# Hybrid attention layer on one core: the output copy on VectorE with three places, and one more key pair as split products

## The chip, the core and the metric

The kernel runs on one core of a Trainium2 chip. The time is the device time of one execution in microseconds (us), median of several runs. Five engines work in parallel, each through its own instructions in order: PE (TensorE, matrix products into the accumulator memory PSUM), DVE (VectorE), ACT (ScalarE), POOL (GpSimd) and SP (SyncE, which issues most DMA transfers). Semaphores tie them together: an instruction that waits holds up everything behind it on its engine.

## The reference, cut to what matters

One transformer layer for 256 prompt tokens and 2048 latent tokens. The change touches only the attention of the latent tokens: 4 heads, each with two softmax maps over 2560 keys (512 cached and 2048 own), whose weighted difference multiplies the values.

```python
s = jnp.einsum('bqhmd,bkhmd->bhmqk', qblk, k).astype(jnp.float32) * scale
p = jax.nn.softmax(s, axis=-1)
a = p[:, :, 0] - lam * p[:, :, 1]
return jnp.einsum('bhqk,bkhe->bqhe', a.astype(v.dtype), v)
```

After it come a norm per head, the output projection and the MLP; a Fourier branch is mixed in before the projection.

## The kernel before, in words

The program passes through stages on the same core: input projection, attention, output projection, a first and a second MLP stage. Attention runs from about 550 to 1255 us of the profiled span.

Attention works on 32 groups, 4 heads times 8 groups of 256 queries. A group has scores (`fill`, L1081, into PSUM tiles Ss of 512 columns), a maximum of each row (`rowmax`, L1086, on DVE, and `comb`, L1089, which joins five of them and negates), the exponentials (`exp`, L1105, on ACT, into P0s and P1s), the weighted difference (`combine`, POOL), and the product with the values. One group of scores takes four steps: two halves j of the queries times two maps m, with five tiles b of 512 keys in each. The products with the values follow six steps behind, so a step computes the scores of one group and the value products of an earlier one.

Value products go by pairs of key tiles: kb = 0, 2, 4, ..., 18 stands for tiles kb and kb + 1. For a pair, PE turns the weights (`tr`, L1136, four transposes into a PSUM tile pts), ACT copies pts to a rounded high part ahs (`ah`, L1143), DVE subtracts that from pts and leaves the low part als (`al`, L1148), and PE multiplies (`mul`): six products of 256 columns per pair (L95, L96, L97: high by high, low by high and high by low, for both tiles) summed in the PSUM tile po. The values Vs stand as a high and a low part as well. Pairs listed in FULL are different: their ahs is a plain fp32 copy, there is no als, and PE takes two fp32 products with unsplit values (vf4s, vf14s; L1162), each recorded as two passes. For pair 14 the first half of the first product runs one step earlier (`mul_part`, L1169).

The four steps of value products take pairs 0, 2 / 4, 6, 8 / 10, 12 / 14, 16, 18; in the two steps with three pairs, the first one is in FULL.

What is shared, and in what turn: the scores have 5 PSUM tiles (Ss), the turned weights 2 (pts), po is one; ahs and als have 4 places each, and the fp32 copies 2 of their own. Places go round in turn, and whoever takes one waits for all readers of what stood in it. So the third `tr` of a step takes the place of the first, and the fifth `ah` that of the first of the last four.

When a group's products are done, `o1` (L1173) copies po to a tile oTs with two places; then follow squares, a power on POOL, two small transfers through memory, a multiplication on POOL and the store to att (L1210). The last group has an oTs of its own in another pool. In the last two groups, turned weights also use the free Ss tiles.

The order is written out by hand: every call is put in a list with a time in units of a step (T, and u = T/5), the list is sorted, and each engine's instructions are recorded in that order. These times set the order only. In a step that begins at w, `rowmax` of the fifth tile stands at 3.9u, `comb` at 4.55u, the third `tr` at 3.86u, `ah` of three pairs at 3.3u, 3.8u and 4.4u, the value products of the step before at 3.9u.

Of the kernel before, what the change touches and what calls it, by code (L numbers as in the profile page):

```python
# [11 lines left out]
F32 = mybir.dt.float32  # L12
# [7 lines left out]
P = 128  # L20
# [9 lines left out]
LAM_INIT = 0.8 - 0.6 * math.exp(-0.3 * 0)  # L30
GRID_W = 64
TSTEP, AVS = 5.2, 6
FULL = (4, 14)

PSCALE = 512 / math.sqrt(256 * 128)

# [5 lines left out]
def body(tc, a, out):  # L42
    nc = tc.nc
    ctx = ExitStack()
    with ctx:
# [944 lines left out]
        with ExitStack() as c3_:  # L990
# [18 lines left out]
            class Head:  # L1009
# [16 lines left out]
                def load_v(self):  # L1026
# [4 lines left out]
                    if not s:  # L1031
                        for kb in FULL:
                            t = ak.tile([P, 2, P], F32, tag=f"vf{kb}", name=f"vf{kb}{self.nm}")
# [6 lines left out]
            class Group:  # L1040
# [98 lines left out]
                def ah(self, kb):  # L1139
                    full = kb in self.hd.vf  # L1140
                    t = at.tile([P, 512], F32 if full else F32R, tag="af" if full else "ah", name=f"ah{self.nm}_{kb}", bufs=2 if full else 4)

                    (nc.vector.tensor_copy if self.drain and kb == FULL[0] else nc.scalar.copy)(t, self.pt[kb])  # L1143
                    self.A[kb] = [t]
# [24 lines left out]
                    nc.tensor.matmul(self.po[:, 0:P], self.hd.vf[kb][:, 0, :], self.A[kb][0][:, 0:P], start=False, stop=False)  # L1169

                def o1(self):
                    self.oT = self.op.tile([P, 256], F32, tag="oT", name=f"oT{self.nm}", bufs=1 if self.last else 2)
                    nc.scalar.copy(self.oT, self.po[:, 0:256])  # L1173

                def oq(self):
                    self.osq = self.op.tile([P, 256], F32, tag="P1_1" if self.hd.s else "osq", name=f"osq{self.nm}", bufs=1)
# [89 lines left out]
            def add(t, fn, *args):  # L1266
                ev.append((t, len(ev), fn, args))
# [20 lines left out]
            for h in range(H):  # L1288
                hd, hp = Head(0, h), Head(1, h)
                base = h * 32 * T  # L1290
                add(base - 18 * T + 0.7 if h else -3.04 * T, hd.load_k)
                add(base - 14 * T + 0.7 if h else 0.9 * T, hd.load_v)
                add(base + 2 * T + 0.7, hp.load_k)
                add(base + 2 * T + 0.71, hp.load_v)
                gp = Prompt(hp, 0)
                G = [base + (AVS + 4 * g) * T for g in range(8)]
                add(G[1] - 3 * T, gp.qload)
                for j in range(2):
                    for m in range(2):
                        for t, fn in ((0.4, gp.scores), (0.85, gp.rowmax), (2.7, gp.exp)):  # L1300
                            add(G[1 + 2 * j + m] + t * u, fn, j, m)
                    add(G[2 + 2 * j] + 8 * u, gp.combine, j)
                for t, fn, *args in ((0.25, gp.tr, 0), (0.9, gp.ah), (1.4, gp.al), (17.0, gp.mul), (20.85, gp.o1), (24.45, gp.oq),
                                     (25.3, gp.o2), (26.0, gp.o5), (26.05, gp.opow), (29.5, gp.o6), (34.0, gp.o7),
                                     (40.2, gp.o8), (43.0, gp.o9)):
                    add(G[5] + t * u, fn, *args)
                for g in range(hd.ng):
                    gr = Group(hd, g)
                    add(base - (4 if h or g > 1 else 3) * T + 0.6 * u if base else -3.03 * T, gr.qload)
                    for st in range(4):  # L1310
                        j, m = divmod(st, 2)
                        t0 = base + st * T
                        for b in range(hd.nbk):
                            add(t0 - T + (0.76 + 0.66 * b) * u, gr.fill, j, m, b)
                            add(t0 - T + (1.26 + 0.66 * b) * u, gr.rowmax, j, m, b)
                            add(t0 + 0.66 * b * u, gr.exp, j, m, b)
                        add(t0 - 0.45 * u, gr.comb, j, m)
                        if m:
                            add(t0 + (4.5 if gr.last and j else 5.9) * u, gr.combine, j)
                            if gr.last and j:  # L1320
                                add(t0 + T + 5.3 * u, gr.combine_v, j)
                    kbs = list(range(0, hd.nkt, 2))
                    for q in range(4):
                        w = base + (AVS + q) * T
                        if q % 2 == 0:
                            order = [kbs.pop(0) for _ in range(2)]
                            tr_t, ah_t, al_t = [0.7, 2.2], [3.3, 3.8], [4.6, 5.2]
                        else:
                            order = [kbs.pop(0) for _ in range(3)]
                            tr_t, ah_t, al_t = [0.7, 2.2, 3.86], [3.3, 3.8, 4.4], [None, 4.6, 5.2]  # L1330
                        for n, kb in enumerate(order):
                            add(w + tr_t[n] * u, gr.tr, kb)
                            add(w + (2.0 if gr.drain and kb == FULL[0] else ah_t[n]) * u, gr.ah, kb)
                            if al_t[n]:
                                add(w + al_t[n] * u, gr.al, kb)
                            add(w + T + (3.9 + 0.01 * n) * u, gr.mul, kb)
                            if q == 3 and not n:
                                add(w + 3.95 * u, gr.mul_part, kb)
                    w = base + (AVS + 5) * T + 1.0 * u
                    for t, fn in ((0, gr.o1), (8.5, gr.oq), (9.3, gr.o2), (10.0, gr.o5), (10.05, gr.opow), (13.0, gr.o6), (17.5, gr.o7), (24.2, gr.o8), (27.0, gr.o9)):  # L1340
                        if gr.last and t > 1:
                            LASTO.append(fn)
                        else:
                            add(w + t * u, fn)
                    base += 4 * T
# [606 lines left out]
        with ExitStack() as c6:  # L1952
# [52 lines left out]
            for i in range(7):  # L2005
                for k in range(16):
                    n = i * 16 + k
# [7 lines left out]
            with tc.manual_schedule():  # L2015
                pend, NM, loaded, KS = None, 7 * 24, 4, []
                for i in range(7):
                    for b in range(3):
                        ps = [pp.tile([P, 512], F32, tag="ps", name=f"ps{i}_{b}_{j}", bufs=6) for j in range(3)]
                        for k in range(16):  # L2020
                            n, m = i * 16 + k, (i * 3 + b) * 8 + k // 2
# [107 lines left out]
```

## Time and profile before

| | |
|---|---|
| median of 3 runs | 2867.51 us (2867.2 to 2867.67) |
| the profiled execution | 2865.04 us |
| its span, first to last instruction | 2863.3 us |
| mean granted clock of PE | 0.998 |
| PE busy | 2830.0 us (99%) |
| DVE busy | 1982.4 us (69%) |
| ACT busy | 1525.3 us (53%) |
| POOL busy | 1068.7 us (37%) |

The span is what the profile's times count in; the time of the execution has about 2 us around it. Busy times of PE hold pipelined instructions, each counted until its modelled end, so 99% does not say that PE never waits: start times of successive instructions tell more. A line of the timeline gives start, duration, engine, source line, operation, output and inputs, count, and in brackets the idle time before it with what ended it.

### The profile page before, as it was taken

What the parts mean: (1) busy time and instruction counts of PE and PEld (TensorE: products, weight loads), DVE (VectorE), ACT (ScalarE), POOL (GpSimd) and SP (SyncE); (2) the same over time, 40 slices, a digit from 0 to 9 for tenths busy, and PEclk for the clock granted to TensorE, in tenths of its full rate; (3) what the DMA queues carried; (4) which work ended last, traced back from release to release, by engine and by line L of the source; (5) the groups of instructions that cost most, each with busy time, mean ns of one, the idle gap of its engine ahead of it and who ended that gap; (6) DMA issues with size and microseconds to landing.
All of it is one profiled execution on the core that took longest, in us unless ns stands there. A gap on an engine that the chain in (4) does not pass through costs nothing.

```text
span 2863.3 us, 43138 instructions
## 1 busy us (share of the span) xinstructions
PE 2830.0 (99%) x15093; PEld 2462.1 (86%) x15093; DVE 1982.4 (69%) x3357; ACT 1525.3 (53%) x3383; POOL 1068.7 (37%) x855
## 2 busy tenths in 40 slices
PE   8999999999999999999999999999999999999999
PEld 5888888688888888888889999999998888888887
DVE  7777786888888888864477777778775354345554
ACT  4333332788888888853356565556555332333221
POOL 1221223789898898942223333333332000000000
PEclk9999999999999999999999999999999999999999
DMA  7777767431222322147767676667747464445663
GB/s 284 215 213 206 234 202 248 159 109 47 78 74 53 112 54 87 46 121 211 246 218 234 221 247 229 220 219 237 235 168 255 146 203 135 137 144 185 207 204 110
DMA packets 404795, 497.69 MB, mean 174 GB/s; under 512 B 31539, under 2 KB 320672, under 8 KB 401506
## 3 DMA queue, kind: packets, MB, share of 16 engines
q1 hardware_dynamic: 399088, 484.35, 53.4%
q0 software_dynamic: 1936, 7.41, 0.8%
q10 hardware_dynamic: 3554, 3.17, 0.3%
q8 instruction: 119, 1.95, 0.3%
q14 instruction: 98, 0.80, 0.1%
HBM read 317.30 MB, written 179.62 MB: 174 GB/s over the span
## 4 chain that ended last, share of the span: by engine, by line
PE 54%; DVE 1%; DMA 0%; issue 0%; ACT 0%; SPq 0%; POOL 0%; DVEq 0%; POOLq 0%
PE ps L95 8%; PE ps L97 8%; PE ps L96 8%; PE pB L1746 2%; PE pB L1745 2%; PE pB L1744 2%; PE pA L1744 2%; PE pC L1746 2%; PE pA L1745 2%; PE pC L1744 2%; PE pC L1745 2%; PE pA L1746 2%; PE po L97 2%; PE po L95 2%; PE po L96 2%; PE pD L1746 1%
## 5 line engine op out<-in xcount | busy, mean ns | idle before, releaser
L1086 DVE TENSOR_REDUCE mxs<-Ss 128x1 f32<-128x512 f32 x636 | 404.9, 685 | 85.5 <-PE Ss L1081 78.2
L1421 DVE TENSOR_TENSOR sl<-sr,sh 128x768 fp32r<-128x768 f32 x168 | 161.8, 964 | 331.6 <-ACT sh L1420 331.1
L1121 POOL TENSOR_TENSOR P0s<-P0s,P1s 128x1024 f32<-128x1024 f32 (+2 forms) x128 | 377.2, 2947 | 10.7
L1420 ACT CAST sh<-sr 128x768 fp32r<-128x768 f32 x168 | 140.6, 838 | 418.3 <-PE ps L96 418.3
L1786 POOL TENSOR_TENSOR gs<-g,g 128x384 f32<-128x384 f32 x48 | 69.7, 1453 | 469.3 <-ACT g L1756 426.4
L1105 ACT ACTIVATE P1s<-Ss,mxs 128x512 f32<-128x512 f32 x318 | 215.4, 694 | 47.7 <-DVE mxs L1089 43.9
L95 PE MATMUL pj<-wh,hh 128*128 128x512 f32 x576 | 228.9, 397 | 2.0 <-DVE hh L556 2.0
L95 PE MATMUL ps<-thT,sh 128*128 128x512 f32 x585 | 227.6, 389 | 0.0
L96 PE MATMUL ps<-tlT,sh 128*128 128x512 f32 x585 | 227.6, 389 | 0.0
L97 PE MATMUL ps<-thT,sl 128*128 128x512 f32 x585 | 227.6, 389 | 0.0
L96 PE MATMUL pj<-wl,hh 128*128 128x512 f32 x576 | 227.3, 395 | 0.1
L97 PE MATMUL pj<-wh,hl 128*128 128x512 f32 x576 | 225.8, 392 | 0.0
L1105 ACT ACTIVATE P0s<-Ss,mxs 128x512 f32<-128x512 f32 x318 | 214.6, 692 | 4.1 <-DVE mxs L1089 4.0
L1136 PE MATMUL pts<-ident,P0s 128*128 128x128 f32 x1280 | 193.4, 275 | 4.8 <-DVE als L1148 1.8
L1081 PE MATMUL Ss<-KS0s,Qs 128*128 128x512 f32 x636 | 188.8, 418 | 4.9 <-ACT P1s L1105 3.7
L1081 PE MATMUL Ss<-KS1s,Qs 128*128 128x512 f32 x636 | 188.1, 419 | 1.8 <-ACT P0s L1105 1.4
L1136 PEld LDWEIGHTS pts<-ident,P0s 128*128 128x128 f32 x1280 | 152.8, 142 | 36.3 <-issue 4.2
L1755 ACT ACTIVATE g<-uz 128x384 f32<-128x384 f32 x144 | 75.8, 526 | 200.2 <-DVE uz L1778 174.1
L1120 POOL TENSOR_SCALAR P1s<-P1s,tots 128x1024 f32<-128x1024 f32 (+2 forms) x128 | 171.5, 1340 | 5.8
L1148 DVE TENSOR_TENSOR als<-pts,ahs 128x512 fp32r<-128x512 f32 x256 | 163.7, 681 | 10.7 <-ACT ahs L1143 10.6
L1143 ACT CAST ahs<-pts 128x512 fp32r<-128x512 f32 x256 | 146.7, 607 | 40.9 <-PE pts L1136 40.9
L95 PE MATMUL ps<-ophT,sh 128*128 128x512 f32 x423 | 164.7, 389 | 1.1 <-DVE uz L1778 1.1
(536 smaller groups left out, 8012.8 us busy)
## 6 DMA issues: line engine op xcount, KB each, us to landing
sr<-sd SPq DMA_DIRECT2D x84, 768.0 KB, 4.3
a<-in_w SPq DMA_DIRECT2D x184, 256.0 KB, 3.6
sd<-gs SPq DMA_DIRECT2D x192, 192.0 KB, 1.9
sd<-g SPq DMA_DIRECT2D x144, 192.0 KB, 4.0
wm<-in_w_mod SPq DMA_DIRECT2D x32, 512.0 KB, 5.2
Qs<-qd SPq DMA_DIRECT2D x32, 512.0 KB, 5.1
b<-in_w SPq DMA_DIRECT2D x64, 256.0 KB, 4.9
b<-tsum SPq DMA_DIRECT2D x64, 256.0 KB, 4.6
```

What stands on the lines that cost most here:

```text
L95: nc.tensor.matmul(ps, lh, rh, start=first, stop=False)
L96: nc.tensor.matmul(ps, lh, rl, start=False, stop=False)
L97: nc.tensor.matmul(ps, ll, rh, start=False, stop=last)
L1081: nc.tensor.matmul(S[:, :w], self.Q[:, x, m, j * P:j * P + P], self.hd.KS[m][:, b * 512:b * 512 + w], start=(x == 0), stop=(x == 1))
L1086: nc.vector.tensor_reduce(self.mx[j][:, m, b:b + 1], self.S[j, m, b], axis=AX.X, op=ALU.max)
L1105: nc.scalar.activation(dst, S, AF.Exp, bias=self.mx[j][:, m, 6:7], accum_out=self.sm[j][:, m, b:b + 1])
L1120: nc.gpsimd.tensor_scalar(p, p, tot[:, 3:4], 0.0, op0=ALU.mult, op1=ALU.add)
L1121: nc.gpsimd.tensor_add(d, d, p)
L1136: nc.tensor.transpose(pt[:, c:c + P], self.p0[j][:, (kb + t) * P:(kb + t + 1) * P], ident)
L1744: nc.tensor.matmul(ps, wh[:, c], hh[:, k, :], start=first and k == 0, stop=False, skip_group_check=True)
L1745: nc.tensor.matmul(ps, wh[:, c], hl[:, k, :], start=False, stop=False, skip_group_check=True)
L1746: nc.tensor.matmul(ps, wl[:, c], hh[:, k, :], start=False, stop=k == 3, skip_group_check=True)
```

## The change

Three edits. The list FULL loses pair 14: tiles 14 and 15 now take the way of the other pairs, with a rounded high part, a low part on DVE (recorded at 4.1u, just ahead of `comb`) and six products; the fp32 values for them are no longer loaded, and the early half product is gone. `o1` moves from ACT to DVE. oTs gets three places (the last group's own stays one).

```diff
-FULL = (4, 14)
+FULL = (4,)
...
                 def o1(self):
-                    self.oT = self.op.tile([P, 256], F32, tag="oT", name=f"oT{self.nm}", bufs=1 if self.last else 2)
-                    nc.scalar.copy(self.oT, self.po[:, 0:256])
+                    self.oT = self.op.tile([P, 256], F32, tag="oT", name=f"oT{self.nm}", bufs=1 if self.last else 3)
+                    nc.vector.tensor_copy(self.oT, self.po[:, 0:256])
...
-                            tr_t, ah_t, al_t = [0.7, 2.2, 3.86], [3.3, 3.8, 4.4], [None, 4.6, 5.2]
+                            tr_t, ah_t, al_t = [0.7, 2.2, 3.86], [3.3, 3.8, 4.4], [4.1 if q == 3 else None, 4.6, 5.2]
...
-                            if q == 3 and not n:
+                            if kb in FULL and q == 3:
                                 add(w + 3.95 * u, gr.mul_part, kb)
```

Over the program this takes out 96 rows of fp32 products of pair 14 on PE and puts in 192 split ones; DVE gains 32 subtractions and 32 copies; ACT loses 32 copies, and 32 plain copies become rounding ones; SP loses 4 loads; POOL's rows stay as they are.

The places, in group 3 of head 0 (pts_3_18 is the tile of turned weights of group 3, pair 18; the brackets name the engines or transfers that an instruction waits for). First PE, in the fourth step of the group's value products: the third `tr` and the products that follow. Before:

```order
L1081 MATMUL Ss_5_1_0_4_6621<-KS0s_5257,Qs_5_6206 128x512 [waits Activation_49]
L1136 MATMUL pts_3_18_6626<-ident,P0s_3_0_5900 128x128 [waits Activation_49]
L95 MATMUL po<-ahs_3_10_6548,Vs_5315 128x256
L95 MATMUL po<-ahs_3_12_6553,Vs_5315 128x256
L1169 MATMUL po<-ahs_3_14_6619,vf14s_5319 128x128
L1136 MATMUL pts_4_0_6658<-ident,P0s_4_0_6201 128x128 [waits DVE_49,PE_49,Pool_49]
L1162 MATMUL po<-ahs_3_14_6619,vf14s_5319 128x128 [waits Activation_49]
L1162 MATMUL po<-ahs_3_14_6619,vf14s_5319 128x256
L95 MATMUL po<-ahs_3_16_6624,Vs_5315 128x256
```

The same place now:

```order
L1081 MATMUL Ss_5_1_0_4_6632<-KS0s_5257,Qs_5_6214 128x512 [waits Activation_49]
L1136 MATMUL pts_3_18_6637<-ident,P0s_3_0_5903 128x128 [waits DVE_49,PE_49]
L95 MATMUL po<-ahs_3_10_6559,Vs_5315 128x256
L95 MATMUL po<-ahs_3_12_6564,Vs_5315 128x256
L1136 MATMUL pts_4_0_6670<-ident,P0s_4_0_6209 128x128 [waits DVE_49,PE_49,Pool_49]
L95 MATMUL po<-ahs_3_14_6630,Vs_5315 128x256 [waits Activation_49]
L96 MATMUL po<-als_3_14_6656,Vs_5315 128x256
L95 MATMUL po<-ahs_3_16_6635,Vs_5315 128x256
```

The turned weights of pair 18, which take the place of those of pair 14, waited for ACT and now wait for DVE, whose subtraction for pair 14 is the last reader. Then DVE in the same step, now:

```order
L1086 TENSOR_REDUCE mxs_5_1_6599<-Ss_5_1_0_4_6632 128x1 [waits PE_49]
L1148 TENSOR_TENSOR als_3_14_6656<-pts_3_14_6594,ahs_3_14_6630 128x512 [waits Activation_49]
L1089 TENSOR_REDUCE mxs_5_1_6599<-mxs_5_1_6599 128x1 [waits DVE_49]
L1148 TENSOR_TENSOR als_3_16_6661<-pts_3_16_6619,ahs_3_16_6635 128x512 [waits Activation_49]
L1148 TENSOR_TENSOR als_3_18_6665<-pts_3_18_6637,ahs_3_18_6658 128x512 [waits Activation_49]
```

The second row is new; the others stood in this order before. Last ACT at the same place, now:

```order
L1143 CAST ahs_3_14_6630<-pts_3_14_6594 128x512 [waits PE_49,Activation_49]
L1143 CAST ahs_3_16_6635<-pts_3_16_6619 128x512 [waits PE_49,Activation_49]
L1143 CAST ahs_3_18_6658<-pts_3_18_6637 128x512 [waits DVE_49,PE_49]
L1105 ACTIVATE P0s_5_1_6663,sms_5_1_6600<-Ss_5_1_0_0_6602,mxs_5_1_6599 128x512 [waits DVE_49]
L1143 CAST ahs_4_0_6710<-pts_4_0_6670 128x512 [waits PE_49,Activation_49]
L1143 CAST ahs_4_2_6717<-pts_4_2_6697 128x512 [waits PE_49,Activation_49]
L1105 ACTIVATE P1s_5_1_0_6741,sms_5_1_6600<-Ss_5_1_1_0_6675,mxs_5_1_6599 128x512 [waits DVE_49,Pool_49]
```

The sequence on ACT is the one before, but with nine users of the four places in a group in place of eight, the high part of pair 18 now takes the place of that of pair 10, and the next group's pair 2 that of pair 14. The last readers of these places are value products on PE: those of pair 10 stand behind the turned weights of pair 18, and those of pair 14 at the end of the next step.

## The prediction

> **What bounds the kernel now.** I read the windows first, then the waits of the attention stage, then the timeline of one step. The windows give busy time per engine (PE, PEld, DVE, ACT, POOL) with the granted clock behind them:
>
> ```profile
> 563.90:1220.40 656.50, 650.44 (x4205) 555.65 (x4204) 554.43 (x1106) 575.30 (x1551) 591.89 (x444) 1.00 0.28 73
> ```
>
> PE is nearly always busy, but DVE, ACT and POOL stand at 84 to 90%: four engines in a ring, each a little behind the next. Who waits for whom there (us in all, times, longest):
>
> ```profile
> PEld Ss L1081 <- ACT P1s L1105: 16.7, 30, 0.6
> PEld Ss L1081 <- ACT P0s L1105: 15.4, 44, 0.5
> ```
> ```profile
> ACT P1s L1105 <- DVE mxs L1089: 43.6, 57, 1.4
> ACT ahs L1143 <- PE pts L1136: 43.0, 69, 2.1
> ACT oTs L1173 <- DMA att<-oTs: 4.2, 1, 4.2
> ```
>
> PE waits for exponentials to free score tiles (32.1 us, 1.0 per group), ACT waits for maxima and for turned weights, DVE for scores. No engine has room that another would not notice, so what counts is how late each event comes in the step that is changed. That step in one group, first DVE:
>
> ```profile
> 901.52 1.29 DVE L1086 TENSOR_REDUCE mxs<-Ss 128x1 f32<-128x512 f32 x2
> 902.84 0.16 DVE L1089 TENSOR_REDUCE mxs<-mxs 128x1 f32<-128x5 f32 x1
> 902.92 1.28 DVE L1148 TENSOR_TENSOR als<-pts,ahs 128x512 fp32r<-128x512 f32 x2
> ```
>
> then ACT:
>
> ```profile
> 902.48 0.59 ACT L1143 CAST ahs<-pts 128x512 fp32r<-128x512 f32 x1 [0.78 <-PE pts L1136]
> 903.04 0.69 ACT L1105 ACTIVATE P0s<-Ss,mxs 128x512 f32<-128x512 f32 x1
> ...
> 906.37 1.09 ACT L1143 CAST ahs<-pts 128x512 fp32r<-128x512 f32 x2
> 908.46 0.69 ACT L1105 ACTIVATE P1s<-Ss,mxs 128x512 f32<-128x512 f32 x1 [1.00 <-DVE mxs L1089]
> ...
> 909.80 0.37 ACT L1173 COPY oTs<-po 128x256 f32<-128x256 f32 x1
> 910.05 0.71 ACT L1105 ACTIVATE P1s<-Ss,mxs 128x512 f32<-128x512 f32 x1
> ```
>
> and PE:
>
> ```profile
> 901.79 0.60 PE L1136 MATMUL pts<-ident,P0s 128*128 128x128 f32 x4
> 902.14 0.37 PE L95 MATMUL po<-ahs,Vs 128*128 128x256 f32 x1
> ...
> 902.83 0.28 PE L97 MATMUL po<-ahs,Vs 128*128 128x256 f32 x1
> ...
> 903.62 0.38 PE L1169 MATMUL po<-ahs,vf14s 128*128 128x128 f32 x2
> 903.84 0.60 PE L1136 MATMUL pts<-ident,P0s 128*128 128x128 f32 x4
> ...
> 907.14 0.81 PE L1162 MATMUL po<-ahs,vf14s 128*128 128x128 f32 x4
> 907.61 0.47 PE L95 MATMUL po<-ahs,Vs 128*128 128x256 f32 x1
> 907.91 0.28 PE L96 MATMUL po<-als,Vs 128*128 128x256 f32 x1
> ...
> 910.90 0.73 PE L1081 MATMUL Ss<-KS0s,Qs 128*128 128x512 f32 x2 [0.19 <-ACT P1s L1105]
> ```
>
> To be seen: PE turns pair 18 at 901.79, while DVE is still in the maxima (to 902.81). ACT waits 0.78 us for those turned weights and starts the exponentials the moment its copy is done; the maximum is ready at the same time (903.00). There is no slack on this path.
>
> **The change part by part.**
>
> *PE's products.* The fp32 products of pair 14 take 903.62 to 903.84 (0.22) and 907.14 to 907.91 less one split product of about 0.12 (0.65): 0.87 us per group. The split products go from 902.14 to 902.83 in five steps, first changeover included, some 0.12 each, so six take 0.70. PE's work falls by 0.17 us a group, 5.4 us in 32. Of that, 0.22 goes away ahead of the transposes at 903.84, and 0.05 is added behind 907.14.
>
> *The place of the turned weights.* Pair 18's four transposes now wait until DVE has subtracted pair 14. That subtraction stands behind the fifth maximum, which ends at 901.52 + 1.29 = 902.81. Two subtractions in 1.28 us, at 0.68 for one, follow each other at 0.60, so it ends near 903.41. How fast PE goes on after DVE in such a case is in the trace: once per head, the prompt's subtraction holds the transposes up in the same way:
>
> ```profile
> 656.00 0.68 DVE L1249 TENSOR_TENSOR alp<-ptp,ahp 128x512 fp32r<-128x512 f32 x1
> ```
> ```profile
> 656.83 0.41 PE L1136 MATMUL pts<-ident,P0s 128*128 128x128 f32 x2 [0.30 <-DVE alp L1249]
> ```
>
> From 656.68 to 656.83 is 0.15. The transposes so start at 903.56 in place of 901.79: **1.77 us late**. Behind them on PE stand all products of pairs 10 and 12, which were ready, and the next transposes and scores.
>
> *The places of the high parts.* ACT's copy for pair 18 must now also wait for the last product of pair 10, which stands behind those transposes: it starts 902.83 − 901.79 = 1.04 later and runs 0.28, so it ends at 904.88. The copy began 0.09 after the transposes' end (902.48 against 901.79 + 0.60), so now at 904.97: **2.49 late**. The exponentials come 0.56 behind, at 905.53. The later maximum (0.60) ends at 903.60 and is no longer what they wait for.
>
> *What follows on PE.* The third score tile of the next step already waits for the third exponential:
>
> ```profile
> 905.21 0.19 PEld L1081 LDWEIGHTS Ss<-KS1s,Qs 128*128 128x128 f32 x1 [0.27 <-ACT P0s L1105]
> ```
>
> so from there PE is 2.49 late too, and its 0.22 us of dropped work at 903.62 disappears in waiting. The maxima follow the scores, so DVE is as late. The products of pair 14 start at 907.14 + 2.49 = 909.63 and their last ends at 909.63 + 5 x 0.12 + 0.28 = 910.51. Only then may ACT copy the next group's pair 2 (place of pair 14): 910.60 in place of 906.37 + 0.47 = 906.84. Much of these 3.8 us was idle time, the 1.00 ahead of 908.46 and the shift: the exponentials start at 911.16 against 908.46 + 2.49 = 910.95, so this adds 0.2. Late by 2.7.
>
> *The output copy.* Off ACT, it lets the third exponential start 0.25 earlier (909.80 to 910.05), and the score tile at 910.90 waits for just that one: **2.4 us late** remains. On DVE the copy comes after the next two subtractions and before the maxima of the next step, where DVE idles:
>
> ```profile
> 910.28 0.69 DVE L1086 TENSOR_REDUCE mxs<-Ss 128x1 f32<-128x512 f32 x1 [0.72 <-PE Ss L1081]
> ```
>
> Its price there isn't in the trace. The small maximum (0.16) and a 512-column subtraction (0.68) bound it; a 256-column operation of DVE in the projection is nearest:
>
> ```profile
> L350 DVE TENSOR_TENSOR qt<-qn,tb x64: 412/418/422, 104.9 to 470.6; 128x256 f32<-128x256 f32 x64
> ```
>
> I take 0.42, less than the 0.72. If that cover were gone, the maxima would come up to 0.4 later per group (13 us in all). Nothing on PE is held by the copy: the next products into po stand a step later.
>
> The remaining two steps of a group are as before, with all engines equally late, POOL a little less; none of them waits for POOL or a transfer there, so nothing is made up. Dropping the four loads of vf14s costs and gains nothing: SP's queue holds nobody up there. The high part of pair 14 as a rounding copy costs what the plain one cost.
>
> *The end of attention.* ACT waits once for an oTs place (4.2 us above); PE stands still, and the clock is halved for one stretch behind it:
>
> ```profile
> 1242.78 0.39 PE L95 MATMUL po<-ahs,Vs 128*128 128x256 f32 x1 [1.94 <-ACT oTs L1173]
> ```
> ```profile
> 1240.24:1243.65 3.41, 1.47 (x13) 1.23 (x12) 0.00 (x0) 1.30 (x4) 0.95 (x2) 1.00 0.23 74
> 1243.65:1247.06 3.41, 3.41 (x17) 3.32 (x17) 1.85 (x3) 1.46 (x4) 0.74 (x1) 0.50 0.13 41
> 540.50:543.91 3.41, 1.78 (x9) 1.09 (x8) 2.07 (x7) 3.41 (x12) 3.33 (x3) 1.00 0.00 0
> 543.91:547.33 3.42, 2.11 (x10) 1.40 (x10) 2.96 (x7) 2.40 (x7) 3.42 (x2) 1.00 0.13 18
> ```
>
> A third place removes both: 1.94 + up to half of 3.41 (1.7), less about 1.0 of added DVE work in the last group: −2.6 us (bounds −4 and +1).
>
> **Sum.** The last two groups have more places for turned weights, so 30 groups are late by 2.4 us: +72. With −2.6 it is +69.4. The profiled execution took 2865.04, so 2934.4; it is 2.5 below the median of the runs (2867.51), so **2937 us**. Per group the bounds are 1.4 (if PE's 1.0 us of waiting absorbed as much) and 2.7 (if the output copy's gain failed): +39 to +78, or 2907 to 2946.
>
> **The clock.** A stretch with 1.47 us of PE work was followed by half clock; one with 1.78 us was not. In the new order the worst 3.41 us hold the stall from the scores' end (901.95) to 903.56, and about 1.8 us of work: just on the safe side. The Trainium skill (TensorE: Matmul & The Clock Gate, section Why this matters for your kernels) says to avoid idle gaps over about 3 us; by it the 1.77 us do nothing, and the sum stays. The rows are stricter, since the recorded gap of 1.94 us was enough. The same page (Part 4: PE-mode transpose) says that transposes don't count as busy in the same way, which fits the row at 1242.78, ahead of which PE only transposed; by that the new stall would look 0.35 us longer and the next rival gain.
>
> **Rivals.**
> 1. *The ring absorbs part.* If the slack in the steps of pairs 0 to 12 makes up the 1.0 us that PE waits per group, 1.4 x 30 − 2.6 = +39: 2907 us. For it: those waits. Against: they are all for exponentials, which are late themselves.
> 2. *The clock halves in many groups.* A halved stretch loses up to 1.7 us of PE work, of which the new waits for exponentials (0.9 per group, by the same working) may hide some. With 0.8 to 1.7 in half to all of 30 groups: +12 to +51 on the forecast, 2949 to 2988.
> 3. *Faster.* If the subtraction of pair 14 ended before 901.79, that is 1.6 us earlier than the row order gives, nothing would be held up: −5.4 of products, −8 (32 x 0.25) of the output copy, −2.6 at the end, 2851 us. Against: DVE has no free time before its fifth maximum, which needs scores that end after 901.79.
> 4. *No change*, if all of it drowned in waits: nothing in the rows speaks for it.
>
> **How the numbers follow.** The forecast 0.70, rival 1 0.12, rival 2 0.12, rival 3 0.04, rival 4 0.02. A measurement here can tell about 0.2% (5.7 us) from no change. So faster by more 0.04, within 0.02, slower 0.94. The range from 2905 to 2962 takes in both bounds, rival 1 and the lower part of rival 2.
>
> **What would show it.** Right: PE's L1136 for pts waits for DVE als L1148, near 1.7 us in each of 30 groups, some 50 us in all; ACT's copies ahs L1143 wait longer, for PE's po products; the period of a group grows by about 2.4 us, all of it between 550 and 1320 us; the wait of 4.2 us for oTs is gone, and the clock is 1.00 throughout attention. Wrong: a period that grows by less than 1.5 (rival 1), a clock below 1.00 there (rival 2), or PE going on at once after the scores (rival 3).

## The result, and the profile after

The changed kernel takes 2931.47 us (median of 4 runs, 2929.14 to 2932.82), the kernel before 2867.36 us: a ratio of 1.0225, 95% interval 1.0213 to 1.0237, 64 us more. The prediction said 2937, between 2905 and 2962. Its mechanism holds; two terms of its sum are off, the groups by 7.8 us too much and the end of attention by 5.2 us too little. That they partly cancel is luck.

The windows of attention of the changed kernel, with the columns of before (time, busy PE, PEld, DVE, ACT, POOL, then granted clock; PEld is PE's loading of weights):

```profile
563.90:1284.00 720.10, 668.01 (x4215) 545.82 (x4216) 584.32 (x1166) 563.80 (x1522) 593.27 (x444) 1.00 0.25 66
```

PE was busy for 99% of this stage and is now for 93%, at the same clock. No other engine took its place: ACT, POOL and DVE are all less busy than before as a share (DVE 81% after 84%). The waits of the stage (550 to 1325 us) say why:

```profile
ACT ahs L1143 <- PE po L97: 125.3, 62, 3.2
PEld pts L1136 <- issue: 61.3, 36, 2.0
PE pts L1136 <- DVE mxs L1089: 48.2, 30, 1.6
PEld Ss L1081 <- ACT P0s L1105: 41.5, 114, 0.6
PEld Ss L1081 <- ACT P1s L1105: 16.6, 56, 0.4
```

Two waits are new and large: ACT's copies wait for products on PE, twice a group (62), and PE's transposes wait for DVE, once a group (30). The waits of PE for exponentials have grown from 32.1 to 58.1 us, since the exponentials themselves come later. One group, DVE first:

```profile
932.15 3.12 DVE L1086 TENSOR_REDUCE mxs<-Ss 128x1 f32<-128x512 f32 x5 [0.74 <-PE Ss L1081]
935.19 0.68 DVE L1148 TENSOR_TENSOR als<-pts,ahs 128x512 fp32r<-128x512 f32 x1
935.79 0.15 DVE L1089 TENSOR_REDUCE mxs<-mxs 128x1 f32<-128x5 f32 x1
...
944.31 0.42 DVE L1173 COPY oTs<-po 128x256 f32<-128x256 f32 x1
945.15 1.29 DVE L1086 TENSOR_REDUCE mxs<-Ss 128x1 f32<-128x512 f32 x2 [0.42 <-PE Ss L1081]
```

then PE and ACT:

```profile
933.24 1.17 PE L1081 MATMUL Ss<-KS0s,Qs 128*128 128x512 f32 x4
936.02 0.63 PE L1136 MATMUL pts<-ident,P0s 128*128 128x128 f32 x4 [1.61 <-DVE mxs L1089]
...
937.07 0.28 PE L97 MATMUL po<-ahs,Vs 128*128 128x256 f32 x1
```
```profile
937.39 0.59 ACT L1143 CAST ahs<-pts 128x512 fp32r<-128x512 f32 x1 [3.23 <-PE po L97]
937.87 0.69 ACT L1105 ACTIVATE P0s<-Ss,mxs 128x512 f32<-128x512 f32 x1
...
942.94 0.59 ACT L1143 CAST ahs<-pts 128x512 fp32r<-128x512 f32 x1 [1.13 <-PE po L97]
943.42 0.69 ACT L1105 ACTIVATE P1s<-Ss,mxs 128x512 f32<-128x512 f32 x1
```

The subtraction of pair 14 runs from 935.19 to 935.87, pair 18's transposes start 0.15 later, pair 10's sixth product ends at 937.35, and ACT's copy starts 0.04 behind that: the chain of the prediction, link by link. The profile puts PE's wait down to L1089, DVE's small maximum, because that ended last on DVE (935.94); the built program says that the subtraction is what it waits for, and the 0.15 fits.

How much a group lost is in the starts of the output copies (durations, then first and last start of those between 925 and 1002 us), before and after:

```profile
L1173 ACT COPY oTs<-po x4: 367/370/371, 932.2 to 999.4; 128x256 f32<-128x256 f32 x4
```
```profile
L1173 DVE COPY oTs<-po x3: 416/417/424, 944.3 to 993.2; 128x256 f32<-128x256 f32 x3
```

That is 22.40 us per group before and 24.45 now. All in all, the copies of the first and the thirtieth group start at 570.31 and 1226.86 before, at 573.04 and 1291.06 now: 64.20 us later at the thirtieth. The last two groups take 25.16 us where they took 27.78. And from the last copy to the end of the program it is 1613.86 us where it was 1608.61. 64.2 − 2.6 + 5.2 is 66.8, the difference of the two spans (2930.1 and 2863.3).

The prediction had nothing for these 5.2 us. In the kernel before, the first product of the output projection came without a gap:

```profile
1254.44 0.39 PE L95 MATMUL po<-woh,mh 128*128 128x512 f32 x1
```

Now PE stands still ahead of it, and the windows there (same columns) show half the clock behind the gap:

```profile
1318.05 0.47 PE L95 MATMUL po<-woh,mh 128*128 128x512 f32 x1 [1.87 <-DVE mh L1573]
```
```profile
1315.95:1319.36 3.41, 1.07 (x5) 0.47 (x5) 3.11 (x5) 2.68 (x6) 1.10 (x2) 1.00 0.20 55
1319.36:1322.77 3.41, 3.41 (x11) 2.76 (x12) 3.41 (x6) 3.41 (x7) 0.00 (x0) 0.50 0.46 96
1322.77:1326.18 3.41, 3.41 (x10) 2.64 (x9) 1.77 (x5) 0.92 (x2) 0.03 (x1) 0.50 0.96 197
```

The gap of 1.87 us and half of the 6.82 us at half clock come to 5.3, which is an estimate from these rows.

### The profile page after: what moved, and what is told of

Read it like the earlier page. It is cut to its first block, busy times and chain, and to the rows that moved or that the text cites. A ratio compares the mean times of both kernels' runs of the same rounds, so it can differ in the third digit from the quotient of the medians.

```text
span 2930.1 us, 43190 instructions
## 1 busy us (share of the span) xinstructions
PE 2847.2 (97%) x15093; PEld 2451.4 (84%) x15093; DVE 2015.1 (69%) x3421; ACT 1512.3 (52%) x3351; POOL 1068.9 (36%) x855
## 4 chain that ended last, share of the span: by engine, by line
PE 52%; DVE 1%; DMA 1%; ACT 0%; issue 0%; SPq 0%; POOL 0%; ACTq 0%; DVEq 0%; POOLq 0%
PE ps L95 8%; PE ps L97 8%; PE ps L96 8%; PE pC L1746 2%; PE pB L1745 2%; PE pB L1746 2%; PE pC L1744 2%; PE pB L1744 2%; PE pC L1745 2%; PE pA L1746 2%; PE pA L1745 2%; PE pA L1744 2%; PE po L97 2%; PE po L95 2%; PE po L96 2%; PE pD L1746 1%
## 5 line engine op out<-in xcount | busy, mean ns | idle before, releaser
L1143 ACT CAST ahs<-pts 128x512 fp32r<-128x512 f32 x288 | 166.7, 604 | 145.7 <-PE po L97 125.3
L1148 DVE TENSOR_TENSOR als<-pts,ahs 128x512 fp32r<-128x512 f32 x288 | 187.8, 682 | 51.7 <-ACT ahs L1143 51.5
L1081 PE MATMUL Ss<-KS1s,Qs 128*128 128x512 f32 x636 | 198.4, 428 | 5.1 <-ACT P0s L1105 5.1
L95 PE MATMUL po<-ahs,Vs 128*128 128x256 f32 x576 | 172.7, 300 | 0.4 <-ACT ahs L1143 0.4
```

The costliest lines, as they stand in the source:

```text
L95: nc.tensor.matmul(ps, lh, rh, start=first, stop=False)
L1081: nc.tensor.matmul(S[:, :w], self.Q[:, x, m, j * P:j * P + P], self.hd.KS[m][:, b * 512:b * 512 + w], start=(x == 0), stop=(x == 1))
L1148: nc.vector.tensor_sub(t, self.pt[kb], f32(self.A[kb][0]))
```

## The experiments

Medians and periods in one table. The period is that of ordinary groups, between the starts of their output copies, and the end goes from the last copy to the last instruction; both come from one profiled execution of each kernel. Each ratio is to the kernel before as run together with that kernel.

| kernel | median us | ratio to before, 95% | period | end |
|---|---|---|---|---|
| before | 2866 to 2867 | | 22.39 | 1608.6 |
| after | 2931.5 | 1.0213 to 1.0237 | 24.47 | 1613.9 |
| split_only | 2941.4 | 1.0245 to 1.0273 | 24.75 | 1609.7 |
| copy_only | 2874.9 | 1.0018 to 1.0039 | 22.12 | 1615.2 |
| places_only | 2879.8 | 1.0035 to 1.0060 | 22.38 | 1613.6 |
| places_pad | 2867.3 | 0.9994 to 1.0012 | 22.38 | 1614.8 |
| copy_pad | 2861.4 | 0.9971 to 0.9989 | 22.12 | 1614.5 |
| copy_2places | 2862.8 | 0.9980 to 0.9997 | 22.12 | 1611.5 |
| after_ah5 | 2909.4 | 1.0137 to 1.0165 | 23.70 | 1614.3 |
| after_tr_late | 2911.4 | 1.0143 to 1.0171 | 23.80 | 1614.1 |
| early5 | 2872.7 | 1.0014 to 1.0032 | 22.55 | 1615.2 |
| after_last_act | 2932.8 | 1.0218 to 1.0246 | 24.48 | 1612.5 |
| after_chain | 2928.8 | 1.0203 to 1.0231 | 24.47 | 1609.2 |
| copy_chain | 2859.5 | 0.9964 to 0.9985 | 22.11 | 1614.2 |

### Which part costs: the split, the copy, the places

The split pair alone (the changed kernel with the old copy):

```diff
-... name=f"oT{self.nm}", bufs=1 if self.last else 3)
-                    nc.vector.tensor_copy(self.oT, self.po[:, 0:256])
+... name=f"oT{self.nm}", bufs=1 if self.last else 2)
+                    nc.scalar.copy(self.oT, self.po[:, 0:256])
```

> Pair 14 split as in the changed kernel, but the output copy stays on ACT with two places. Theory A (the two new waits of the split pair, for DVE ahead of pair 18's transposes and for PE ahead of ACT's copies, cost all of the 64 us, and the copy on DVE gives 0.25 us a group back): slower than the changed kernel, 2931.5 + 31 x 0.25 (the copy) + 2.6 (the wait for an oTs place is back) - 3 (the first products of the output projection no longer stand behind the copy) = about 2939 us, period 24.7 us. Theory B (the copy on DVE, in the middle of its row of maxima, is a good part of the cost): 2920 us or less, period below 24.2 us.

2941.4 us; the copies of ACT, between 925 and 1002 us:

```profile
L1173 ACT COPY oTs<-po x3: 377/378/381, 949.1 to 998.7; 128x256 f32<-128x256 f32 x3
```

24.8 us a group. Theory A stands: the split pair costs all of the loss, and the copy on DVE gives 0.28 us a group of it back.

The copy on DVE with three places, in the kernel before. To make room for the third place, the fp32 copies of turned weights (tag af) get one place instead of two:

```diff
-... tag="af" if full else "ah", ... bufs=2 if full else 4)
+... tag="af" if full else "ah", ... bufs=1 if full else 4)
...
-... name=f"oT{self.nm}", bufs=1 if self.last else 2)
-                    nc.scalar.copy(self.oT, self.po[:, 0:256])
+... name=f"oT{self.nm}", bufs=1 if self.last else 3)
+                    nc.vector.tensor_copy(self.oT, self.po[:, 0:256])
```

> The kernel before with the output copy on DVE and three places for it (the fp32 copies of turned weights get one place in place of two to make room). Theory A: the third exponential starts 0.25 us earlier in each group, 31 x 0.25 = -7.8; the wait for a place is gone, -2.6; but the last group's copy now stands on DVE ahead of the split of the output projection's first operand (mh, ml), about 2.1 us of PE waiting and up to 1 of clock, +3: about 2860 us. Theory B: 0.42 us of DVE delays the maxima in each group, 30 x 0.42 = +13: about 2880 us.

And three places alone, the same diff without the line of the copy:

> The kernel before with three places for oTs, copy on ACT as before (fp32 copies of turned weights with one place to make room). Theory A: the one wait of 4.2 us on ACT, PE's gap of 1.94 us and the half clock behind it are gone: -2.6, between -4 and -1, about 2865 us. Rival: ACT's copy was released just when something else would have held PE anyway: no change.

Both came out slower, 2874.9 and 2879.8. For places_only no theory had that. For copy_only theory B had forecast 2880, but from slower groups, and that is not what happened: the period fell to 22.12, as theory A has it, and with three places alone it is 22.38. The loss lies in one place, at the start of attention (places_only, ACT and PE):

```profile
534.34 0.69 ACT L1105 ACTIVATE P0s<-Ss,mxs 128x512 f32<-128x512 f32 x1 [15.99 <-DMA four<-ys]
```
```profile
535.17 2.07 PE L1081 MATMUL Ss<-KS1s,Qs 128*128 128x512 f32 x4 [13.07 <-ACT P0s L1105]
```

The first exponential waits 16 us for a store of the stage before. The edit had made the pool of turned weights 1 KB smaller in each partition, so the tiles behind it moved. The wait says that P0s came to lie on a tile that was still being stored. So both were repeated with 1 KB of padding in that pool (`shift(at, 1152, "a")` for `shift(at, 128, "a")`), and the copy also with nothing else changed:

> As copy_only, but with 1 KB of padding in the pool of turned weights, so that the tiles behind it lie where they lie in the kernel before. Theory A (the 13 us at the start of attention in copy_only and places_only, an exponential that waits for a store of the stage before, come only from the exponentials' tiles having moved by 1 KB onto the stored tile): this wait is gone, the period is 22.12 us as in copy_only against 22.39, 31 x 0.27 = -8.4; at the end -3.8 for the place and +6.6 behind it: about 2860.5 us. Theory B (the single place for the fp32 copies is what costs 13 us): 2875 us again.

> The kernel before with the output copy on DVE and nothing else: two places, no tile moved. Theory A (the third place is worth nothing, since what it gains in the last groups is lost behind them, where the output projection waits for the prompt's output through memory): -8.4 from the copy and nothing else: about 2858 us, the end of attention to the end of the program about 1608.7 us as in the kernel before. Rival (without the third place DVE itself waits 4 us for a store, with the subtractions and maxima of the last groups behind it): 2861 us or more.

> The kernel before with three places for oTs and the copy on ACT, with the tiles behind the pool left where they were (1 KB of padding). Theory A (the third place takes 2.6 to 3.8 us from the last two groups and gives 5 us back behind them, where the output projection then waits for the prompt's output through memory): no change, 2866 to 2869 us; groups at 22.39, the last two 12.7 and 11.2 us, from the last copy to the end 1613.6 us; no wait of 13 us at the start of attention. Theory B (the prediction's term: the third place is worth 2.6 us): 2863.7 us.

copy_pad took 2861.4, copy_2places 2862.8, places_pad 2867.3 us. So the 13 us were the layout: the single place for the fp32 copies is still there, and they are gone. The copies of copy_pad:

```profile
L1173 DVE COPY oTs<-po x4: 415/415/416, 929.4 to 995.7; 128x256 f32<-128x256 f32 x4
```

22.10 us a group: the copy on DVE gains 0.27 to 0.3 us in each. The third place alone, with the copy on ACT, changes nothing that can be measured (0.9994 to 1.0012), against the 2.6 us of theory B. In places_pad the last two groups take 24.0 us instead of 27.8, and behind them PE waits (DVE's and PE's waits from 1225 to 1262 us):

```profile
DVE mh L1573 <- DMA wout<-att: 3.7, 1, 3.7
PE po L95 <- DVE mh L1573: 3.1, 1, 3.1
```

The first operand of the output projection (mh) is the prompt's attention output, which goes through memory, and that does not come sooner because ACT's copy does. With two places (copy_2places) the stall stays where it was, on DVE now, and PE's gap with it:

```profile
1235.56 0.42 DVE L1173 COPY oTs<-po 128x256 f32<-128x256 f32 x1 [3.33 <-DMA att<-oTs]
```
```profile
1236.13 0.48 PE L95 MATMUL po<-ahs,Vs 128*128 128x256 f32 x1 [2.07 <-DVE oTs L1173]
```

Its 2862.8 is what the rival said (2861 or more), and theory A (2858) is wrong for it: DVE does wait for the store, and from the last copy to the end it takes 1611.5 us and not 1608.7. With the copy on DVE the third place so brings 1.4 us in the medians, which can hardly be told from the spread of the runs (2861.1 to 2867.5 with two places, 2859.3 to 2863.9 with three); the profiled spans are alike, 2859.4 and 2859.6.

### What in the split costs

Five places for the high parts, so that ACT waits for no product (nothing moves in memory, the two edits cancel):

```diff
-... tag="af" if full else "ah", ... bufs=2 if full else 4)
+... tag="af" if full else "ah", ... bufs=1 if full else 5)
```

> The changed kernel with five places for the high parts instead of four (one instead of two for the fp32 copies, so nothing moves in memory). Pair 18's copy on ACT no longer waits for the products of pair 10, and the next group's pair 2 no longer for those of pair 14; pair 18's transposes on PE still wait for DVE. Theory A (what counts is how late ACT's copy and the exponentials behind it come; PE's own stall is slack): the copy comes 0.7 us earlier after the transposes, the second wait (0.13) goes too: period 24.47 - 0.8 = 23.7, 30 x 0.8 = -24: about 2908 us. Theory B (the stall of 1.6 us on PE ahead of the transposes sets the period): less than 0.2 per group, 2925 us or more.

The other way round, the third `tr` of the step behind the products of pairs 10 and 12, four places as in the changed kernel:

```diff
-tr_t, ah_t, al_t = [0.7, 2.2, 3.86], ...
+tr_t, ah_t, al_t = [0.7, 2.2, 3.95 if q == 3 else 3.86], ...
```

> The changed kernel with pair 18's transposes recorded behind the products of pairs 10 and 12 instead of ahead of them: PE has 1.43 us of ready work in the place of its stall, the transposes start when DVE is done (about as now), and the place for ACT's copy is already free. Theory A (lateness of ACT's copy and the exponentials counts): like five places, the copy 0.7 us earlier: period 23.7 to 23.8, about 2909 us. Theory B (PE's stall counts): 1.4 us per group come back, period 23.0, 30 x 1.4 = -42: about 2889 us.

2909.4 and 2911.4 us, within 2.5 of theory A in both. after_ah5, PE and ACT:

```profile
924.03 0.63 PE L1136 MATMUL pts<-ident,P0s 128*128 128x128 f32 x4 [1.60 <-DVE mxs L1089]
```
```profile
924.75 0.59 ACT L1143 CAST ahs<-pts 128x512 fp32r<-128x512 f32 x1 [2.57 <-PE pts L1136]
```

and after_tr_late:

```profile
924.82 1.29 PE L1136 MATMUL pts<-ident,P0s 128*128 128x128 f32 x8 [0.20 <-DVE mxs L1089]
```
```profile
925.49 0.59 ACT L1143 CAST ahs<-pts 128x512 fp32r<-128x512 f32 x1 [2.52 <-PE pts L1136]
```

In the first, PE stands still for 1.60 us, in the second for 0.20 us; their times differ by 2 us. What they share is ACT's copy, 0.72 and 0.67 us behind the start of the transposes where it was 1.37. PE's stall as such costs next to nothing: in after_tr_late PE waits for the exponentials a little later instead (0.69 us). What the ring keeps is the lateness of the copy, and of the exponentials behind it. The periods differ by 0.1 (23.70 and 23.80), and after_tr_late still has the second wait of ACT for products, worth 0.13, which five places take away.

Then the rest, the lateness of the transposes: five places, and pair 14's copy and subtraction earlier in ACT's and DVE's order:

```diff
-[3.3, 3.8, 4.4], [4.1 if q == 3 else None, 4.6, 5.2]
+[2.3 if q == 3 else 3.3, 3.8, 4.4], [2.5 if q == 3 else None, 4.6, 5.2]
```

> The changed kernel with five places for the high parts (as after_ah5), and pair 14's high part recorded one exponential earlier on ACT and its subtraction on DVE after the second maximum of the step instead of after the fifth. The transposes of pair 18 then find their place free when PE comes to them; but the last three maxima come one subtraction (0.60 us) later. Theory A (what is left of the loss in after_ah5, 23.7 against 22.12 us with the copy on DVE, is the wait of pair 18's transposes for DVE): no stall on PE ahead of them, period 22.12 + 0.6 = 22.7 us, about 2909 - 30 x 1.0 = 2879 us. Rival (a split pair costs DVE and ACT so much that the ring stays slow wherever it stands): period 23.2 or more, 2894 us or more.

2872.7 us: 59 of the 64 us are back, and it is 6 us faster than theory A's 2879. The subtraction now stands between the second and the third maximum, the thirty stalls of 1.6 us on PE are gone (no wait of `tr` for DVE is over 0.5 us), and the period is 22.55:

```profile
925.88 0.68 DVE L1148 TENSOR_TENSOR als<-pts,ahs 128x512 fp32r<-128x512 f32 x1
926.48 0.68 DVE L1086 TENSOR_REDUCE mxs<-Ss 128x1 f32<-128x512 f32 x1
```
```profile
L1173 DVE COPY oTs<-po x3: 417/424/425, 935.0 to 980.1; 128x256 f32<-128x256 f32 x3
```

Theory A had forecast 22.7, with all of the 0.60 us by which the maxima come later; 22.55 is 0.43 over copy_pad, which has pair 14 in fp32 (22.12). ACT now waits for the maximum before the exponentials:

```profile
928.59 0.69 ACT L1105 ACTIVATE P0s<-Ss,mxs 128x512 f32<-128x512 f32 x1 [0.48 <-DVE mxs L1089]
```

That fits the 0.43, but no run takes this wait away, so that it is the cause is argued and not shown. Against copy_pad (2861.4), the split pair so costs 70 us in the changed kernel: 22 go with the fifth place, 37 more with the earlier copy and subtraction, and 11 stay.

### The 5 us behind attention

The last group's copy alone back on ACT:

```diff
-                    nc.vector.tensor_copy(self.oT, self.po[:, 0:256])
+                    (nc.scalar.copy if self.last else nc.vector.tensor_copy)(self.oT, self.po[:, 0:256])
```

> The changed kernel, with the last group's output copy alone back on ACT. Theory A (the 5.2 us that the profile of the changed kernel loses behind the end of attention come from DVE: the last copy waits for PE's last product and the split of the first operand of the output projection, mh and ml, stands behind it): the first product of the projection starts about 1.4 us earlier and the stretch of half clock behind it shrinks or goes: -1.4 to -4, about 2928.5 us. Rival (the 5.2 us come from ACT, whose copy of the last pair stands behind four weight copies): less than 0.5 us gained, 2931 us.

2932.8 us: no gain in the median, where theory A had 2928.5, though the end is 1.4 us shorter (1612.5). mh no longer stands behind the copy, but now it waits for its data:

```profile
1318.95 0.69 DVE L1573 CAST mh<-wout 128x1024 fp32r<-128x1024 f32 x1 [0.60 <-DMA wout<-att]
```

These data come through a chain on SP. In the changed kernel (SP's own row of issues):

```profile
1295.75 0.32 SPq L1196 DMA_DIRECT2D rs<-ossp  x1
1304.75 0.32 SPq L1210 DMA_DIRECT2D att<-oTs  x1
1305.18 0.37 SPq L1201 DMA_DIRECT2D rbp<-rs  x1
```

The prompt's factors leave at 1295.75, and their load comes 9.4 us later, because it stands behind a store that waits for POOL. The load was put ahead of that store, in the last head only, with the copy of the last group on ACT as above:

```diff
-(34.0, gp.o7)
+(30.0 if h == H - 1 else 34.0, gp.o7)
```

> The changed kernel with the same two edits for its end. Theory A: from the last copy to the end of the program 1609 us instead of 1613.9 (after) or 1612.4 (after_last_act): about 2928 us. Rival: 2932 us, as after_last_act.

2928.8 us, and the end is 1609.2, as forecast (2928 and 1609). The first product of the projection:

```profile
1319.27 0.47 PE L95 MATMUL po<-woh,mh 128*128 128x512 f32 x1 [0.50 <-DVE mh L1573]
```

The clock stays at 1.00 behind it. So both causes were real, one behind the other: the copy in DVE's row ahead of mh, and behind it SP's chain. This rests on the ends of profiled executions, 4.7 us apart; the medians, 2.6 us apart, hardly tell the two kernels apart by themselves (1.0203 to 1.0231 against 1.0213 to 1.0237). In the profile of after_chain attention also starts later, with the first output copy at 575.46 and not at 573.04, behind a stretch of half clock at 544 us. The same edits on copy_pad:

> copy_pad with two more edits for the end of attention: the last group's copy stays on ACT, and in the last head SP issues the load of the prompt's factors (rbp) ahead of the store of a group's output that it stood behind. Theory A (behind attention the first product of the output projection waits for mh, the prompt's output through memory, whose chain on SP stood behind a store that waits for POOL, and behind the last copy on DVE): the chain comes 3 us earlier, the gap of 2.5 us on PE and the slower clock behind it go, from the last copy to the end of the program 1608.7 us as in the kernel before instead of 1614.5: about 2855.6 us. Rival (the weights' copies on ACT or their subtraction on DVE hold the first products anyway): 2860 us.

2859.5 us, the lowest median here, though its interval overlaps that of copy_pad. Theory A failed: the end is 1614.2 and not 1608.7, and the time is the rival's (2860). But the rival's cause is not it either. The wait only moved on: the first product comes at once, and the second token tile waits for its transfer (waits from 1230 to 1260 us):

```profile
DVE mh L1573 <- DMA mT<-four: 3.2, 1, 3.2
PE po L95 <- DVE mh L1573: 2.5, 1, 2.5
```

## Why the prediction was right, and where it was off

- **PE's products**, 0.17 us less work a group (5.4 in all), were to disappear in waiting, and the sum had nothing for them. No run tests that by itself; after_ah5 and after_tr_late show the same for a larger amount, 1.4 us of PE's stall in a group that makes no difference.
- **The transposes**, 1.77 late: from the scores' row, PE could have gone on at 933.24 + 1.17 − 0.16 = 934.25 (the 0.16 is the overlap of the rows before, 901.95 against 901.79); it did at 936.02. 1.77 measured.
- **The places of the high parts**, the copy 1.41 behind the start of the transposes: 1.37 measured. The exponentials came 0.48 behind it and not 0.56: in the rows before they also waited for the maximum, which had long been there now.
- **The next pair**, +0.2: from the first to the second set of exponentials it is 5.55 (937.87 to 943.42) against 5.42 before, so 0.13.
- **The output copy**: 0.42 us on DVE, as taken, hidden ahead of the next maxima, where DVE still idles for 0.42; the gain is 0.27 to 0.28 per group, against 0.25.
- **The sum per group** was the first mis-sized term: 2.4 forecast, 2.1 measured (64.2 over 30 groups; 72 was forecast). The differences above come to about 0.2; the other 0.1 is not accounted for. Rival 1, which had the ring take up 1.0, is out.
- **The end of attention** is the term that failed. "A third place removes both" was true of ACT's wait and of PE's gap, and the last two groups did win 2.6 us; but nobody asked what is late next. The output projection could not start earlier than the prompt's output comes through memory, and the copy on DVE stood ahead of mh in DVE's row. In place of −2.6 stands +2.6 (−2.6 + 5.2).
- **The number**: 2937 is 5.5 us above the measured 2931.5. The groups give 7.8 of that and the end takes 5.2 back, by luck. The other 2.9 lie in the step from span to median: the profiled execution before was 2.5 below its median, which the prediction added, and the one now is 0.4 above its own.
- **The clock**: 1.00 in the groups, as forecast; rival 2 is out. The reason given, that about 1.8 us of work in 3.41 is on the safe side, is not borne out by the other runs (last section), so that part was luck. A window around the stall has 1.81 us of PE work in 3.41 and is followed by 1.00:

```profile
932.60:936.01 3.41, 1.81 (x10) 1.18 (x10) 3.41 (x8) 1.56 (x4) 3.41 (x2) 1.00 0.00 0
936.01:939.42 3.41, 3.19 (x23) 2.59 (x23) 1.45 (x4) 2.03 (x6) 0.34 (x2) 1.00 0.02 0
```

## What to carry to other kernels

In a ring of engines like this one, an instruction that is made to wait costs what the engines behind it become late, not what its own engine idles: here 1.4 us less of idle PE gained nothing, and 0.7 us of a late copy on ACT did count. When work moves into a ring of places, count the users of each ring per round: a ninth user of four places made ACT wait for PE twice a group, and a fifth place, with one fewer elsewhere, brought 22 us back. And for each stall that a change removes, name what is late next: at the end of attention three stalls stood one behind the other, and taking away the first gained nothing.

## What the runs showed of the hardware

A gap of 1.87 us on PE, in a stretch with 1.07 us of work out of 3.41, was followed by a clock of 0.50 for 6.8 us, while thirty stalls of 1.6 us, with 1.81 us of work out of 3.41 around one of them, left it at 1.00. The Trainium skill (TensorE: Matmul & The Clock Gate, section Why this matters for your kernels) speaks of idle gaps over about 3 us; the stalls in the groups agree, the gap at the end, which is shorter, does not, and there the trace decides.

Neither the length of the gap nor the share of work in such a stretch gives a limit that fits all runs. In after_chain a stretch with 1.77 us of PE work and gaps of 0.38 and 1.36 us is followed by half clock; in after_ah5 one with 1.57 us and a gap of 1.84 us is not. The windows of each run are laid at whole steps of 3.41 us from where its clock changes:

```profile
540.89:544.30 3.41, 1.77 (x6) 0.59 (x4) 3.04 (x7) 3.41 (x11) 3.26 (x2) 1.00 0.01 2
544.30:547.71 3.41, 3.31 (x10) 2.78 (x11) 1.49 (x4) 3.41 (x11) 3.33 (x3) 0.50 0.00 0
```
```profile
544.87:548.28 3.41, 1.57 (x11) 1.02 (x9) 3.12 (x6) 2.39 (x7) 3.23 (x4) 1.00 0.28 92
548.28:551.70 3.42, 3.42 (x20) 2.46 (x19) 2.59 (x5) 3.42 (x10) 3.34 (x2) 1.00 0.18 68
```

What decides between them is open. That transposes count less as work, which the prediction weighed, does not explain it: the first stretch has none. In after_tr_late a stretch with 2.40 us of work, 1.91 of it transposes (658.74 to 662.15 us), is followed by 1.00.

That a tile moved by 1 KB can cost 13 us was not expected either: here its place decided that it had to wait for a store of the stage before.
